# Strassen's identity in the second product of six feed-forward blocks, with the residual in DRAM meanwhile

## Chip, cores and metric

One core of a Trainium2 chip runs the whole kernel. The metric is the device time of one execution in microseconds (us), as the median of several runs. Engines: PE multiplies matrices (PEld loads its weights), DVE, ACT and POOL work elementwise, SP only issues DMAs.

## The reference

Two layers over a sequence of 1024 frames with 1024 channels, float32: layer 0 mixes with a convolution, layer 1 with retention, and each is followed by a feed-forward part. The change lies in the feed-forward part of layer 1:

```
h = modulate(rmsnorm(x, norm_mlp_g[i]), sh2, sc2)
x = x + g2[:, None, :] * (jnp.square(jax.nn.relu(h @ mlp_w1[i])) @ mlp_w2[i])
...
return rmsnorm(x, final_norm_g)
```

mlp_w1 is 1024 x 4096, mlp_w2 is 4096 x 1024, g2 is a gain for each channel.

## The kernel before

x lies in SBUF transposed: `self.x[n][t]` holds 128 channels (n = 0 to 7) by 512 frames (t = 0, 1, the halves of the sequence). To keep float32's precision every operand is split into a high part, rounded to fp32r, and a low part, the rest. `mm3` (L253) multiplies two such operands by three matmuls with 512 columns: high by high, high by low, low by high.

The hidden 4096 channels are worked in eight blocks `fb` of 512. `mlp` (L417) does for each block two products. The first: for each of four hidden tiles f, one weight block of 128x1024 (`block`, L235: a DMA of 512 KB to a raw tile on SP's queue, a cast to the high part on ACT, L245, and a subtraction for the low part on DVE, L246, both into whl tiles), then for each half 8 x 3 matmuls into one PSUM tile, Relu on ACT (L432), the square on DVE (L434), and the split into a packed hid tile (`split_pack`, L276: ACT L281, DVE L282). The second: for each pair np_ of output tiles one weight block, and for each of the two tiles and each half 4 x 3 matmuls into a PSUM tile, which DVE multiplies by g2 and adds to x in SBUF (L454).

`run` (L1160) calls `mlp` for layer 1 three times: block 0 for the first half of the frames, while the second half's retention ends (L1191); the norm of the second half (L1195) and blocks 1 to 7 for both halves (L1196); and block 0 for the second half, with the final norm of both halves and the stores of the output (L1207). Layer 0's feed-forward part uses the same weight layout through `layer_conv`, `mlp` and `mlp_split`.

A scheduler orders this part when the kernel is built: it lists the instructions of each engine by estimated durations and by the place in the program, so an engine may take a later instruction that is ready before an earlier one that is not; on the chip each engine runs its list in that order. A tile waits for a free buffer of its tag: raw 2, tmp 4, whl 8, hB 16, hid0 and hid1 5 each in this part, x0 and x1 8 each (x itself), PSUM 6 for products. A raw tile is free when the cast and the subtraction have read it.

Of the kernel before, what the change touches and what calls it, by code (L numbers as in the profile page):

```python
# [6 lines left out]
F32 = mybir.dt.float32  # L7
F32R = mybir.dt.float32r
BF16 = mybir.dt.bfloat16
AF = mybir.ActivationFunctionType  # L10
ALU = mybir.AluOpType
PSUM = bass.MemoryType.PSUM

P = 128
D = 1024
S = 1024
HALF = 512
KT = D // P
# [7 lines left out]
MID = HALF // 2  # L26

VEC = {}


def _vec_layout():
# [175 lines left out]
class Trunk:  # L207
# [209 lines left out]
    def mlp(self, layer, sched, h, g2, mid=None, split=None):  # L417
        nc, io = self.nc, self.io
        for fb, halves in sched:
            hid = {t: [] for t in halves}  # L420
            for f in range(4):
                w = self.block(io["w1"][layer, fb * 4 + f])
# [19 lines left out]
            for np_ in range(4):  # L442
                w = self.block(io["w2"][layer, fb, np_])
                if self.bg:
                    self.bg.pop(0)()
                for n2 in range(2):
                    n = np_ * 2 + n2
                    for t in halves:
                        ps = self.psum()
                        for kt in range(4):  # L450
                            o = kt * 256 + n2 * P
                            self.mm3(ps, w, o, hid[t][kt], kt == 0, kt == 3)
                        x = self.x[n][t]
                        nc.vector.scalar_tensor_tensor(x, ps, g2[:, n : n + 1], x, ALU.mult, ALU.add)  # L454

    def mlp_split(self, layer, fb, t, hid, g2, done):

        nc = self.nc
        ws = [self.block(self.io["w2"][layer, fb, np_]) for np_ in range(4)]
        for cs in (slice(0, MID), slice(MID, HALF)):  # L460
            for n in range(KT):
                ps = self.psum()[:, :MID]
                for kt in range(4):
                    o = kt * 256 + n % 2 * P
                    self.mm3(ps, ws[n // 2], o, [a[:, cs] for a in hid[kt]], kt == 0, kt == 3)
                x = self.x[n][t][:, cs]
                nc.vector.scalar_tensor_tensor(x, ps, g2[:, n : n + 1], x, ALU.mult, ALU.add)
            done(t, cs)


    def layer_conv(self):
# [324 lines left out]
        def mlp(fb, p):  # L796
# [15 lines left out]
            for np_ in range(4):  # L812
                name = ("w2", fb, np_)
                for n in (2 * np_, 2 * np_ + 1):
                    ps, x = ("psw", fb, n), ("y", n, 0)
                    for kt in range(4):
                        mm(ps, name, kt * 256 + n % 2 * P, hid[kt], kt == 0, kt == 3, p)
                    op("V", 0.663, p, lambda ps=ps, x=x, n=n: nc.vector.scalar_tensor_tensor(
                        E[x][:, :HALF], E[ps], c1(("modb", 5), n), E[x][:, :HALF], ALU.mult, ALU.add), r=[ps, ("modb", 5)], w=[x])

# [339 lines left out]
    def run(self):  # L1160
# [22 lines left out]
        with tc.tile_pool(name="ret", bufs=1, reuse_waits="tile") as rp, tc.tile_pool(name="dp", bufs=1, space=bass.MemoryType.DRAM) as dp:  # L1183
# [5 lines left out]
            hm = {0: h0}  # L1189
            self.hidtag = {0: ["q", "k"]}  # L1190
            self.mlp(1, [(0, [0])], hm, g2, mid=out)  # L1191
        with tc.tile_pool(name="g1", bufs=1, reuse_waits="tile") as gp:
            self.tags.update(whl=(gp, 8), hB=(gp, 16), hid0=(gp, 5), hid1=(gp, 5))
            self.hidtag = {0: ["hid0"], 1: ["hid1"]}
            hm[1] = self.norm(1, G2, sh2, "hB")  # L1195
            self.mlp(1, [(fb, [0, 1]) for fb in range(1, 8)], hm, g2)  # L1196

            def first():
                self.tagname = {"tmp": "hid0", "xg": "hA"}
# [38 lines left out]
def lay_out(i):  # L1238
# [11 lines left out]
    def kblocks(w):  # L1250

        k, nn = w.shape
        return w.reshape(k // 512, 4, P, 4, 256).transpose(0, 3, 2, 1, 4).reshape(k // 512, 4, P, 1024)

    vec = np.zeros((P, NVEC), np.float32)

    def put(name, a):
# [26 lines left out]
        "rgate": c(ktiles(win[:, 4096:], 0)),  # L1284
        "rout": c(kblocks(i["ret_w_out"][0])),
        "w1": c(np.stack([ktiles(w, 0) for w in i["mlp_w1"]])),
        "w2": c(np.stack([kblocks(w) for w in i["mlp_w2"]])),
    }
    d.update(constants_np())
    return d  # L1290
# [23 lines left out]
```

## Time and profile before

| | |
|---|---|
| median of 3 runs | 2702.75 us (2698.78 to 2705.78) |
| profiled execution | 2705.48 us |
| span of its trace | 2703.6 us |
| PE busy | 2613.8 us, 97% of the span, 11450 matmuls |
| DVE busy | 1635.2 us, 60% |
| ACT busy | 1068.3 us, 40% |
| POOL busy | 314.5 us, 12% |
| mean granted clock of PE | 0.985 of full speed |

Busy shares are means over the whole span. Matmuls are pipelined, so one matmul's own duration is longer than the distance to the next one. Blocks 1 to 7 of layer 1 fill the span from about 2026 to 2640 us. Durations of elementwise operations are in ns for one instruction; "idle before" is how long the engine had nothing to do ahead of these instructions, and behind the arrow stands what ended the wait.

### The profile page before, as it was taken

The numbers are of one execution on the slowest core, as the hardware profiler recorded it, in microseconds if no ns is written. First come the engines' busy times: TensorE is split into PE (matmuls) and PEld (weight loads), VectorE is DVE, ScalarE is ACT, GpSimd is POOL, SyncE is SP. The second block draws the span as 40 slices with busy tenths as digits, with TensorE's granted clock in tenths as the row PEclk, the third lists the DMA queues.
The fourth block names the chain that finished last, engine by engine and source line by source line (L and its number), as shares of the span: only waits on it lengthen the run. The fifth ranks groups of instructions, "written<-read, shape, count | busy, mean of one in ns | idle before, by whom it ended". The sixth has DMA issues, their size and how long they took to land.

```text
span 2703.6 us, 29259 instructions
## 1 busy us (share of the span) xinstructions
PE 2613.8 (97%) x11450; PEld 2119.2 (78%) x11450; DVE 1635.2 (60%) x2237; ACT 1068.3 (40%) x1582; POOL 314.5 (12%) x212
## 2 busy tenths in 40 slices
PE   2989999999999999999999999999999999999997
PEld 1756777888787888788888888888888888888886
DVE  7799999965577445645545655365565333333336
ACT  4656866463222323343433633433543211222124
POOL 3677439100000000000000000000000000000002
PEclk6999999999999999999999999999999999999999
DMA  7522322242376223322222232232222111111112
GB/s 253 203 71 86 109 93 87 93 128 98 119 233 217 96 94 96 115 86 94 71 94 94 71 103 85 71 101 86 78 70 71 48 54 47 47 47 47 48 54 86
DMA packets 77197, 259.66 MB, mean 96 GB/s; under 512 B 8577, under 2 KB 11009, under 8 KB 76930
## 3 DMA queue, kind: packets, MB, share of 16 engines
q1 hardware_dynamic: 74240, 252.98, 28.6%
q10 hardware_dynamic: 2818, 4.81, 0.5%
q8 instruction: 90, 1.47, 0.2%
q14 instruction: 49, 0.40, 0.0%
HBM read 251.46 MB, written 6.29 MB: 95 GB/s over the span
## 4 chain that ended last, share of the span: by engine, by line
PE 84%; DVE 7%; DMA 4%; ACT 2%; issue 2%; POOL 1%; DVEq 0%; ACTq 0%; SPq 0%; POOLq 0%
PE mm L260 25%; PE mm L259 25%; PE mm L258 25%; DMA araw<-ada 3%; PE mm L964 2%; PE mm L963 2%; PE mm L962 2%; DVE acc L733 1%; POOL cacc L741 1%; DVE whl L523 1%; DVE araw L319 1%; PE ax L606 1%; PE acc L721 1%; DVE araw L555 0%; DVE hid L555 0%
## 5 line engine op out<-in xcount | busy, mean ns | idle before, releaser
L245 ACT CAST whl<-raw 128x1024 fp32r<-128x1024 f32 x264 | 277.0, 1050 | 809.7 <-PE mm L259 472.3
L246 DVE TENSOR_TENSOR whl<-raw,whl 128x1024 fp32r<-128x1024 f32 x264 | 322.7, 1223 | 403.5 <-ACT whl L245 302.7
L258 PE MATMUL mm<-hA,whl 128*128 128x512 f32 x1200 | 483.2, 403 | 44.5 <-ACT whl L522 41.7
L260 PE MATMUL mm<-hA,whl 128*128 128x512 f32 x1200 | 475.5, 396 | 8.5 <-DVE whl L523 6.3
L259 PE MATMUL mm<-hA,whl 128*128 128x512 f32 x1200 | 476.1, 397 | 1.9 <-DVE hA L542 1.7
L258 PE MATMUL mm<-hid,whl 128*128 128x512 f32 (+1 forms) x1024 | 394.3, 386 | 4.6 <-ACT hid L281 3.0
L259 PE MATMUL mm<-hid,whl 128*128 128x512 f32 (+1 forms) x1024 | 392.8, 384 | 1.1 <-DVE hid L282 1.0
L260 PE MATMUL mm<-hid,whl 128*128 128x512 f32 (+1 forms) x1024 | 392.8, 384 | 0.0
L258 PEld LDWEIGHTS mm<-hA,whl 128*128 128x128 f32 x1200 | 227.7, 190 | 101.3 <-ACT whl L522 43.5
L258 PE MATMUL mm<-hB,whl 128*128 128x512 f32 x704 | 279.3, 397 | 0.0
L260 PEld LDWEIGHTS mm<-hA,whl 128*128 128x128 f32 x1200 | 227.5, 190 | 63.8 <-DVE whl L523 9.8
L259 PE MATMUL mm<-hB,whl 128*128 128x512 f32 x704 | 274.4, 390 | 0.0
L260 PE MATMUL mm<-hB,whl 128*128 128x512 f32 x704 | 274.2, 390 | 0.0
L259 PEld LDWEIGHTS mm<-hA,whl 128*128 128x128 f32 x1200 | 227.6, 190 | 58.7 <-issue 5.3
L454 DVE SCALAR_TENSOR_TENSOR x<-mm,modb,x 128x512 f32<-128x512 f32 x192 | 143.8, 749 | 211.6 <-PE mm L260 211.0
L741 POOL TENSOR_TENSOR cacc<-cacc,prod 128x512 f32<-128x512 f32 x166 | 253.4, 1529 | 112.9 <-ACT prod L738 57.9
L1143 POOL TENSOR_SCALAR hA<-x,vec 128x256 f32<-128x256 f32 (+1 forms) x12 | 7.5, 622 | 2164.3 <-DVE x L454 2143.8
L258 PEld LDWEIGHTS mm<-hid,whl 128*128 128x128 f32 x1024 | 192.9, 189 | 45.6 <-ACT hid L281 5.9
L259 PEld LDWEIGHTS mm<-hid,whl 128*128 128x128 f32 x1024 | 192.9, 188 | 41.3 <-DVE hid L282 2.9
L260 PEld LDWEIGHTS mm<-hid,whl 128*128 128x128 f32 x1024 | 193.1, 189 | 37.1
L733 DVE SCALAR_TENSOR_TENSOR acc<-x,vec,acc 128x512 f32<-128x512 f32 x239 | 166.8, 746 | 2.8 <-PE acc L721 1.9
L259 PEld LDWEIGHTS mm<-hB,whl 128*128 128x128 f32 x704 | 132.2, 188 | 31.3 <-issue 2.9
(233 smaller groups left out, 3776.3 us busy)
## 6 DMA issues: line engine op xcount, KB each, us to landing
raw<-w SPq DMA_DIRECT2D x192, 512.0 KB, 3.5
araw<-ada SPq DMA_DIRECT2D x80, 512.0 KB, 4.3
raw<-pw SPq DMA_DIRECT2D x38, 512.0 KB, 4.1
raw<-rqk SPq DMA_DIRECT2D x32, 512.0 KB, 3.5
raw<-rv SPq DMA_DIRECT2D x32, 512.0 KB, 3.5
raw<-rgate SPq DMA_DIRECT2D x32, 512.0 KB, 3.5
raw<-rout SPq DMA_DIRECT2D x32, 512.0 KB, 3.5
x<-x SPq DMA_DIRECT2D x32, 256.0 KB, 3.2
```

Source lines behind the costliest of these rows:

```text
L245: nc.scalar.copy(hi[i], raw[:, i * W : i * W + W])
L246: nc.vector.tensor_tensor(lo[i], raw[:, i * W : i * W + W], hi[i].bitcast(F32), ALU.subtract)
L258: nc.tensor.matmul(out, whi, rhi, start=start, stop=False)
L259: nc.tensor.matmul(out, whi, rlo, start=False, stop=False)
L260: self.last_mm = nc.tensor.matmul(out, wlo, rhi, start=False, stop=stop)
L319: i = nc.vector.scalar_tensor_tensor(raw, raw, 1.0, self.cond, ALU.mult, ALU.mult, accum_out=out)
L454: nc.vector.scalar_tensor_tensor(x, ps, g2[:, n : n + 1], x, ALU.mult, ALU.add)
L733: op("V", 0.68, p, lambda s=s, a=a: nc.vector.scalar_tensor_tensor(E[a], sl(s), wv(s), E[a], ALU.mult, ALU.add), r=[u], w=[a])
L741: op("G", 1.28, p, lambda pr=pr: nc.gpsimd.tensor_tensor(E[ca], E[ca], E[pr], ALU.add), r=[pr], w=[ca])
L962: nc.tensor.matmul(vps[jt], hh[0], wh, start=kt == 0, stop=False)
L963: nc.tensor.matmul(vps[jt], hh[0], wl, start=False, stop=False)
L964: nc.tensor.matmul(vps[jt], hh[1], wh, start=False, stop=kt == KT - 1)
```

## The change

For blocks 1 to 6 of layer 1 `mlp` is replaced by `mlp_seven`; block 7 and block 0 stay as they were.

- The second product of a pair of output tiles (n1, n2) is a product of 2 x 2 parts: the weights by output tile and by parity kj of the hidden tile, the hidden values by kj and by half of the frames. Strassen's identity in Winograd's form does it with seven products (`seven`) in place of eight. Each is summed over the two pairs p of hidden tiles, 2 x 3 matmuls into one PSUM tile.
- `pair_weights` makes the seven weight parts from one raw block: four sums and differences of 256 columns on DVE, and the high and low parts in four whl tiles (A11, A12, S1, S2 in one couple, S4, S3, A22 in the other). It replaces `block` there.
- In the first product both Relu (in place in PSUM) and Square are on ACT, the result going to an x0 tile. Of each p's four results (kj, t) it packs seven operands: B11, T1, B21, B22, T2, T3, T4, with four differences on DVE.
- The seven products are gathered with g2 into a tmp tile and three ev tiles: two activations on ACT and eight operations on DVE for each pair. The four sums are added to the residual by accumulating DMAs from POOL's queue into sixteen DRAM tiles xd of 256 KB.
- Ahead of block 1, x is stored to xd from SP's queue; after block 6 it is loaded again, the first half into x0 tiles, the second into halves of four hid0 tiles. In between, x1 tiles hold half of the second half's h.
- Buffers in this part: hB 8, hid0 14 (no hid1), q2 1, ev 6.
- w2's columns lie in another order in DRAM for both layers (`kpairs`, and `o2` in the readers); bytes and DMAs are the same.

```diff
+def o2(kt, n):
+    return (n % 2 * 4 + kt % 2 * 2 + kt // 2) * P
...
+    def pair_weights(self, ap):
+        nc = self.nc
+        tt = nc.vector.tensor_tensor
+        raw = self.t2("raw", cols=1024)
+        nc.sync.dma_start(raw, ap)
+        a11, a12, a21, a22 = (raw[:, i * 256 : i * 256 + 256] for i in range(4))
+        ph, pl, qh, ql = (self.t2("whl", dt=F32R, cols=1024) for _ in range(4))
+        q = self.t2("q2")
+        tt(q[:, 256:], a11, a21, ALU.subtract)
+        nc.scalar.copy(qh[:, 512:768], a22)
+        tt(ql[:, 512:768], a22, qh[:, 512:768].bitcast(F32), ALU.subtract)
+        tt(a21, a21, a22, ALU.add)
+        tt(a22, a21, a11, ALU.subtract)
+        tt(q[:, :256], a12, a22, ALU.subtract)
+        nc.scalar.copy(ph, raw)
+        tt(pl, raw, ph.bitcast(F32), ALU.subtract)
+        nc.scalar.copy(qh[:, :512], q)
+        tt(ql[:, :512], q, qh[:, :512].bitcast(F32), ALU.subtract)
+        p, q = (ph, pl), (qh, ql)
+        return dict(A11=(p, 0), A12=(p, 256), S1=(p, 512), S2=(p, 768), S4=(q, 0), S3=(q, 256), A22=(q, 512))
+
+    def seven(self, np_, w, hid, g2, xd):
+        nc = self.nc
+        n1, n2 = 2 * np_, 2 * np_ + 1
+        g = lambda n: g2[:, n : n + 1]
+        def prod(a, k):
+            ps = self.psum()
+            wt, o = w[a]
+            for p in range(2):
+                self.mm3(ps, wt, o + p * P, hid[p][k], p == 0, p == 1)
+            return ps
+        def plus(ps, n, e, new=False):
+            o = self.t2("ev") if new else e
+            nc.vector.scalar_tensor_tensor(o, ps, g(n), e, ALU.mult, ALU.add)
+            return o
+        def done(n, t, e):
+            nc.gpsimd.dma_start(xd[n][t], e, accum_op=ALU.add)
+        ps = prod("A11", "B11")
+        a, b = self.t2("tmp"), self.t2("ev")
+        nc.scalar.activation(a, ps, AF.Copy, scale=g(n1))
+        nc.scalar.activation(b, ps, AF.Copy, scale=g(n2))
+        done(n1, 0, plus(prod("A12", "B21"), n1, a, True))
+        ps = prod("S2", "T2")
+        plus(ps, n1, a)
+        plus(ps, n2, b)
+        m5 = prod("S1", "T1")
+        plus(m5, n1, a)
+        plus(prod("S4", "B22"), n1, a)
+        done(n1, 1, a)
+        plus(prod("S3", "T3"), n2, b)
+        done(n2, 1, plus(m5, n2, b, True))
+        plus(prod("A22", "T4"), n2, b)
+        done(n2, 0, b)
+
+    def mlp_seven(self, layer, fbs, h, g2, xd):
+        nc, io = self.nc, self.io
+        tt = nc.vector.tensor_tensor
+        for fb in fbs:
+            hid = []
+            for p in range(2):
+                f = {}
+                ops = {}
+                pack = lambda k, src: ops.update({k: self.split_pack(src, "hid0")})
+                for kj in range(2):
+                    w = self.block(io["w1"][layer, fb * 4 + 2 * p + kj])
+                    for t in range(2):
+                        ps = self.psum()
...
+                        nc.scalar.activation(ps, ps, AF.Relu)
+                        sq = f[kj, t] = self.t2("x0")
+                        nc.scalar.activation(sq, ps, AF.Square)
+                        if (kj, t) == (0, 0):
+                            pack("B11", sq)
+                        elif (kj, t) == (0, 1):
+                            tt(f[0, 0], sq, f[0, 0], ALU.subtract)
+                            pack("T1", f[0, 0])
+                        elif (kj, t) == (1, 0):
+                            pack("B21", sq)
+                        else:
+                            pack("B22", sq)
+                            tt(f[0, 0], sq, f[0, 0], ALU.subtract)
+                            pack("T2", f[0, 0])
+                            tt(f[0, 1], sq, f[0, 1], ALU.subtract)
+                            pack("T3", f[0, 1])
+                            tt(f[1, 0], f[1, 0], f[0, 0], ALU.subtract)
+                            pack("T4", f[1, 0])
+                hid.append(ops)
+            for np_ in range(4):
+                self.seven(np_, self.pair_weights(io["w2"][layer, fb, np_]), hid, g2, xd)
...
-            self.tags.update(whl=(gp, 8), hB=(gp, 16), hid0=(gp, 5), hid1=(gp, 5))
-            self.hidtag = {0: ["hid0"], 1: ["hid1"]}
-            hm[1] = self.norm(1, G2, sh2, "hB")
-            self.mlp(1, [(fb, [0, 1]) for fb in range(1, 8)], hm, g2)
+            self.tags.update(whl=(gp, 8), hB=(gp, 8), hid0=(gp, 14), q2=(gp, 1), ev=(gp, 6))
+            self.hidtag = {t: ["hid0"] for t in range(2)}
+            xd = [[xp.tile([P, HALF], F32, name=self.nm("xd"), tag=f"xd{n}_{t}") for t in range(2)] for n in range(KT)]
+            r = self.norm_rstd(1)
+            h = []
+            for kt in range(KT):
+                nc.sync.dma_start(xd[kt][1], self.x[kt][1])
+                h.append(self.norm_h(1, kt, r, G2[:, kt : kt + 1], sh2[:, kt : kt + 1], "hB" if kt < 4 else "x1"))
+            hm[1] = h
+            for kt in range(KT):
+                nc.sync.dma_start(xd[kt][0], self.x[kt][0])
+            self.mlp_seven(1, range(1, 7), hm, g2, xd)
+            xl = [self.t2("hid0", cols=2 * HALF) for _ in range(4)]
+            for kt in range(KT):
+                self.x[kt][0] = self.t2("x0")
+                nc.sync.dma_start(self.x[kt][0], xd[kt][0])
+            for kt in range(KT):
+                self.x[kt][1] = xl[kt // 2][:, kt % 2 * HALF : kt % 2 * HALF + HALF]
+                nc.sync.dma_start(self.x[kt][1], xd[kt][1])
+            self.mlp(1, [(7, [0, 1])], hm, g2)
```

## Rows read from the trace of the kernel before

**Rows 1.** The head of the page and its busy times: busy us, share of the span, number of instructions of each engine.

```profile
span 2703.6 us, 29259 instructions
PE 2613.8 (97%) x11450; PEld 2119.2 (78%) x11450; DVE 1635.2 (60%) x2237; ACT 1068.3 (40%) x1582; POOL 314.5 (12%) x212
```

**Rows 2.** The table of stretches for three successive blocks, each cut into its first and its second product: stretch and length, busy us (and instructions) of each engine, granted clock of PE, busy share of the DMA engines, GB/s.

```profile
core 0: us, PE busy (x) PEld busy (x) DVE busy (x) ACT busy (x) POOL busy (x), PEclk, DMA share, GB/s
2115.06:2159.24 44.18, 44.18 (x193) 36.04 (x192) 15.07 (x19) 12.45 (x19) 0.00 (x0) 1.00 0.15 48
2159.24:2202.77 43.53, 43.53 (x194) 36.04 (x193) 17.36 (x21) 5.29 (x6) 0.00 (x0) 1.00 0.15 49
2202.77:2246.95 44.18, 44.18 (x193) 36.04 (x192) 15.05 (x19) 12.45 (x19) 0.00 (x0) 1.00 0.15 48
2246.95:2290.48 43.53, 43.53 (x194) 36.05 (x193) 17.35 (x21) 5.29 (x6) 0.00 (x0) 1.00 0.15 49
```

**Rows 3.** The same table for the instructions on hid tiles alone, in one second product.

```profile
2159.24:2202.77 43.53, 43.52 (x192) 35.85 (x191) 0.68 (x1) 0.62 (x1) 0.00 (x0) 1.00 0.15 49
```

**Rows 4.** PE's waits from 2000 to 2540 us, the one row of that answer: who waited for whom, us in total, times, the longest.

```profile
PE mm L260 <- DVE whl L246: 0.7, 1, 0.7
```

**Rows 5.** Groups of instructions on DVE and ACT from 2100 to 2537 us, shapes apart: busy us and mean ns of one, then idle time before them.

```profile
L454 DVE SCALAR_TENSOR_TENSOR x<-mm,modb,x 128x512 f32<-128x512 f32 x79 | 59.3, 750 | 123.1 <-PE mm L260 122.8
L246 DVE TENSOR_TENSOR whl<-raw,whl 128x1024 fp32r<-128x1024 f32 x40 | 49.0, 1225 | 73.7 <-ACT whl L245 71.5
L245 ACT CAST whl<-raw 128x1024 fp32r<-128x1024 f32 x40 | 41.9, 1048 | 248.6 <-PE mm L259 248.6
L282 DVE TENSOR_TENSOR hid<-tmp,hid 128x512 fp32r<-128x512 f32 x40 | 27.6, 691 | 24.0 <-ACT hid L281 24.0
L281 ACT CAST hid<-tmp 128x512 fp32r<-128x512 f32 x40 | 24.8, 621 | 43.0 <-DVE tmp L434 43.0
L432 ACT ACTIVATE tmp<-mm 128x512 f32<-128x512 f32 x40 | 23.8, 596 | 58.2 <-PE mm L260 58.2
```

**Rows 6.** The same view from 2600 to 2704 us, the end of the run: operations with 256 columns, and two on 512 columns from SBUF.

```profile
L1132 DVE TENSOR_TENSOR hid<-hid,hid 128x256 f32<-128x256 f32 x12 | 5.2, 437 | 0.7 <-ACT hid L1125 0.2
L1125 ACT ACTIVATE hid<-x 128x256 f32<-128x256 f32 x16 | 6.4, 412 | 13.8 <-DVE x L467 12.9 <-DVE hid L1132 0.7
L1151 DVE TENSOR_TENSOR hA<-hA,rs 128x512 f32<-128x512 f32 x5 | 6.3, 1319 | 0.0
L1132 DVE TENSOR_TENSOR hid<-hid,hid 128x512 f32<-128x512 f32 x7 | 5.1, 733 | 1.6 <-PE mm L260 0.7 <-ACT hid L1125 0.6
```

**Rows 7.** DVE's instructions in order of time around the end of a first product (at 2159.24): start, us, instruction, and in brackets the idle time before it and who ended it.

```profile
2156.06 0.69 DVE L282 TENSOR_TENSOR hid<-tmp,hid 128x512 fp32r<-128x512 f32 x1 [0.69 <-ACT hid L281]
2160.30 1.23 DVE L246 TENSOR_TENSOR whl<-raw,whl 128x1024 fp32r<-128x1024 f32 x1 [3.55 <-ACT whl L245]
2161.44 0.68 DVE L434 SCALAR_TENSOR_TENSOR tmp<-mm,tmp 128x512 f32<-128x512 f32 x1
2162.17 0.75 DVE L454 SCALAR_TENSOR_TENSOR x<-mm,modb,x 128x512 f32<-128x512 f32 x1
2162.84 0.68 DVE L282 TENSOR_TENSOR hid<-tmp,hid 128x512 fp32r<-128x512 f32 x1
```

**Rows 8.** ACT's instructions in the same stretch.

```profile
2159.22 1.05 ACT L245 CAST whl<-raw 128x1024 fp32r<-128x1024 f32 x1 [3.19 <-PE mm L259]
2160.17 0.59 ACT L432 ACTIVATE tmp<-mm 128x512 f32<-128x512 f32 x1
2162.16 0.62 ACT L281 CAST hid<-tmp 128x512 fp32r<-128x512 f32 x1 [1.40 <-DVE tmp L434]
```

**Rows 9.** DMA issues of the whole run by line: tiles, issuing queue, count, KB each, median us from issue to landing.

```profile
raw<-w SPq DMA_DIRECT2D x192, 512.0 KB, 3.5
std<-tmp SPq DMA_DIRECT2D x8, 256.0 KB, 2.0
tmp<-std SPq DMA_DIRECT2D x8, 256.0 KB, 2.6
```

**Rows 10.** The table of stretches where the first half's block 0 ends (to 2026) and the norm of the second half is made.

```profile
2004.00:2026.00 22.00, 22.00 (x98) 18.02 (x96) 9.29 (x12) 4.61 (x5) 0.00 (x0) 1.00 0.15 48
2026.00:2050.00 24.00, 23.35 (x100) 18.24 (x99) 21.91 (x31) 14.79 (x22) 0.00 (x0) 1.00 0.32 100
```

**Rows 11.** The longest wait of SP's queue from 2000 us on: the next weight load waits until DVE has read the raw tile.

```profile
SPq L239 <- DVE whl L246: 632.6, 65, 15.7
```

**Rows 12.** POOL's groups over the whole run: operations on two SBUF tiles of 512 columns.

```profile
L741 POOL TENSOR_TENSOR cacc<-cacc,prod 128x512 f32<-128x512 f32 x166 | 253.4, 1529 | 112.9 <-ACT prod L738 57.9 <-ACT cacc L738 43.7
L1151 POOL TENSOR_TENSOR hA<-hA,rs 128x512 f32<-128x512 f32 x3 | 4.7, 1593 | 27.7 <-DVE rs L374 27.7
```

More of the change, by code (lines that the diff above doesn't have):

```diff
@@ L450, in mlp @@
                         for kt in range(4):
-                            o = kt * 256 + n2 * P
-                            self.mm3(ps, w, o, hid[t][kt], kt == 0, kt == 3)
+                            self.mm3(ps, w, o2(kt, n), hid[t][kt], kt == 0, kt == 3)
                         x = self.x[n][t]
                         nc.vector.scalar_tensor_tensor(x, ps, g2[:, n : n + 1], x, ALU.mult, ALU.add)
+    def pair_weights(self, ap):
[18 more added lines that the diff above has]
+        return dict(A11=(p, 0), A12=(p, 256), S1=(p, 512), S2=(p, 768), S4=(q, 0), S3=(q, 256), A22=(q, 512))
@@ new lines, in mlp_seven @@
+    def mlp_seven(self, layer, fbs, h, g2, xd):
[12 more added lines that the diff above has]
+                        for kt in range(KT):
+                            self.mm3(ps, w, kt * P, h[t][kt], kt == 0, kt == KT - 1)
+                        nc.scalar.activation(ps, ps, AF.Relu)
[19 more added lines that the diff above has]
+                self.seven(np_, self.pair_weights(io["w2"][layer, fb, np_]), hid, g2, xd)
@@ L463, in mlp_split @@
                 for kt in range(4):
-                    o = kt * 256 + n % 2 * P
-                    self.mm3(ps, ws[n // 2], o, [a[:, cs] for a in hid[kt]], kt == 0, kt == 3)
+                    self.mm3(ps, ws[n // 2], o2(kt, n), [a[:, cs] for a in hid[kt]], kt == 0, kt == 3)
                 x = self.x[n][t][:, cs]
@@ L816, in mlp @@
                     for kt in range(4):
-                        mm(ps, name, kt * 256 + n % 2 * P, hid[kt], kt == 0, kt == 3, p)
+                        mm(ps, name, o2(kt, n), hid[kt], kt == 0, kt == 3, p)
                     op("V", 0.663, p, lambda ps=ps, x=x, n=n: nc.vector.scalar_tensor_tensor(
@@ L1191, in run @@
             self.mlp(1, [(0, [0])], hm, g2, mid=out)
+        xp = ctx.enter_context(tc.tile_pool(name="xd", bufs=1, space=bass.MemoryType.DRAM))
         with tc.tile_pool(name="g1", bufs=1, reuse_waits="tile") as gp:
-            self.tags.update(whl=(gp, 8), hB=(gp, 16), hid0=(gp, 5), hid1=(gp, 5))
-            self.hidtag = {0: ["hid0"], 1: ["hid1"]}
-            hm[1] = self.norm(1, G2, sh2, "hB")
-            self.mlp(1, [(fb, [0, 1]) for fb in range(1, 8)], hm, g2)
+            self.tags.update(whl=(gp, 8), hB=(gp, 8), hid0=(gp, 14), q2=(gp, 1), ev=(gp, 6))
[14 more added lines that the diff above has]
+                nc.sync.dma_start(self.x[kt][0], xd[kt][0])
+            for kt in range(KT):
+                self.x[kt][1] = xl[kt // 2][:, kt % 2 * HALF : kt % 2 * HALF + HALF]
+                nc.sync.dma_start(self.x[kt][1], xd[kt][1])
+            self.mlp(1, [(7, [0, 1])], hm, g2)
             def first():
@@ L1253, in kblocks, with kpairs @@
         return w.reshape(k // 512, 4, P, 4, 256).transpose(0, 3, 2, 1, 4).reshape(k // 512, 4, P, 1024)
+    def kpairs(w):
+        k, nn = w.shape
+        return w.reshape(k // 512, 2, 2, P, 4, 2, P).transpose(0, 4, 3, 5, 2, 1, 6).reshape(k // 512, 4, P, 1024)
     vec = np.zeros((P, NVEC), np.float32)
@@ L1286, in lay_out @@
         "w1": c(np.stack([ktiles(w, 0) for w in i["mlp_w1"]])),
-        "w2": c(np.stack([kblocks(w) for w in i["mlp_w2"]])),
+        "w2": c(np.stack([kpairs(w) for w in i["mlp_w2"]])),
     }
```

## Prediction

> **What bounds the kernel now.** I read first the page's line of busy times: PE is busy 97% of the span, DVE 60%, ACT 40%, POOL 12% [rows 1]. An average over unlike stages prices nothing, so the next view is the table of stretches, cut where a block's first product ends and its second ends [rows 2]. Three successive blocks look alike: 44.18 us for the first product, 43.53 us for the second, PE busy for all of both at granted clock 1.00. DVE works 15.1 and 17.4 us in them, ACT 12.5 and 5.3 us, POOL nothing, and the DMA engines are 0.15 busy at 48 GB/s. The same table for the instructions on the hid tiles alone counts 192 matmuls in the second product [rows 3], so one matmul costs 43.53/192 = 226.7 ns there; the first product has as many, at 44.18/192 = 230.1 ns. Last, the waits: in the 540 us from 2000 on PE waited once, 0.7 us [rows 4], while DVE's additions to x wait for PE [rows 5]. In these blocks the time is the count of matmuls and nothing else; the question is whether the new side work stays under PE.
>
> **What is removed.** A pair of output tiles takes 2 x 2 x 4 x 3 = 48 matmuls now and 7 x 2 x 3 = 42 afterwards: seven products, each over the two halves of the hidden block, three matmuls each. Per block 168 for 192, over six blocks 144 fewer: 144 x 0.2267 = **-32.7 us**. The second product becomes 168 x 0.2267 = 38.1 us, the block 82.3 us for 87.7, one pair 9.52 us, one product 1.36 us. Bound on the rate: products of 6 matmuls instead of 12 could run at the first product's 230.1 ns, 168 x 3.4 ns x 6 = 3.4 us; at or below the old rate costs 0. I take the middle, **+1.7**.
>
> **DVE and ACT.** Durations by form are in [rows 5]; the 256-column ones come from the tail of the run [rows 6]. On DVE a block has, in the first product, 4 weight subtractions at 1.225, 14 low halves of packs at 0.691 and 8 differences (nearest row the same 0.691) = 20.1 us. A pair's weights need five 256-column operations at 0.43 (four differences or sums and one low half), one of 1.225 and one of 0.69 = 4.1 us. A pair's results need eight evacuations at 0.750 = 6.0 us. Together 20.1 + 4 x 10.1 = 60.5 us of 82.3, 73%. ACT: 4 x 1.05 + 16 x 0.6 + 14 x 0.621 + 4 x (0.41 + 1.05 + 0.62) + 8 x 0.6 = 35.6 us, 43%; Relu written back to PSUM is in no row, and I take L432's 0.596. So neither is the bound over a block. It is tight inside the second product: 4 x 6.0 + 3 x 4.1 + 2 x 1.225 = 38.7 us of DVE against 38.1 of PE, if no pair is prepared earlier than it must be. It can be: the eight whl tiles hold two pairs, the first pair fits into the first product, and A11, A12, S1 and S2 of a pair are let go after its fourth product, so a pair's weights are wanted some 13 us after they can begin. Moving one pair's 4.1 us gives 34.6. Cost 0; the cover is DVE's idle time in the first product, and if it were gone the 0.6 us per block would cost 3.6 us in all.
>
> **The handover from first to second product.** The part most likely to cost. Now the last hidden tile is ready 4.3 us after its last matmul: the first product ended at 2159.24, ACT took a weight cast first and began the Relu at 2160.17, DVE ended the last low half at 2163.52 [rows 7, 8]. The first 12-matmul group and three quarters of the second hid that. Afterwards the chain is Relu 0.6, Square 0.6, difference 0.69, copy 0.62, low half 0.69 = 3.2 us, up to 5.0 with the 0.93 us of the cast and B22's 0.69 ahead and some 0.2 of hand-overs, up to 6.8 if DVE's weight subtraction and one more low half come between. PE wants T2's second half after two products and three matmuls, 3.4 us, or 4.8 us if S1*T1, ready long before, is issued ahead of S2*T2. So 0 to 3.4 us per block. I take 0.7, near the low end because a product with ready operands exists and the order is laid out from estimated durations: **+4.2** in six blocks (bounds 0 and 20.4).
>
> **The residual in DRAM.** 16 accumulating DMAs of 256 KB per block, issued from POOL, which otherwise does nothing here. No row shows an accumulating DMA or any issued from POOL. 48 GB/s at share 0.15 [rows 2] is 320 GB/s at full share, so a plain 256 KB transfer occupies the engines 0.82 us: the lower bound. The upper one is a load and a store of the same size that follow one another to the landing, 2.6 + 2.0 = 4.6 us [rows 9]. I take a read and a write side by side, 1.6 us, nearer the low end because successive DMAs go to different tiles and nothing makes one wait for another. Neither end reaches the path. On average 16 x 4.6 = 73.6 us fit into 82.3. Inside the second product the six ev tiles come round after two pairs, and the latest, n2's sum, must land within 19.0 + 1.4 - 9.5 = 10.9 us. With 4.6 us one after another the fourth pair finds two tiles 4.4 and 3.6 us late; DVE stands there, with the later evacuations and weight work queued behind it, and PE goes on over the free ones of six PSUM tiles, some four products or 5.4 us. Cost 0. The Trainium skill, Collectives: The Full Stack, section The bandwidth ceiling, says that an add in the DMA path reads two sources and so runs at half a copy's rate; no row here shows it. By it a DMA would take some 1.6 us as an estimate, and the sum would stay as it is.
>
> **Entry and exit.** The norm of the second half is hidden today: in the 24 us from 2026 PE lost 0.65 us [rows 10] while DVE was busy 21.9. Sixteen stores of 256 KB join SP's queue among the weight loads, and half of h waits for x1 tiles to be stored. SP waits only for free raw tiles [rows 11], so it has room. Bounds 0 and two stores in a row, 4.0 us; I take **+1.0**, nearer 0 since x is final up to 20 us before h is made. At the exit SP holds sixteen loads behind the last accumulations; a weight block is wanted each 11 us with two raw tiles ahead, and x itself only at the second product, 44 us later. Bounds 0 and 4.6, taken **+1.0**.
>
> **Sum.** -32.7 + 1.7 + 4.2 + 1.0 + 1.0 = -24.8 us. The profiled execution took 2705.48 us (span 2703.6), 2.7 above the median of 2702.75. 2705.5 - 24.8 = 2680.7 for an execution like it, and **2678** for the median.
>
> **Rivals.** *Eaten up:* all bounds at their upper ends, handovers 20.4, rate 3.4, entry 4.0, exit 4.6, together 32.4: -0.3, about 2702. For it: the handover chain grows while its cover shrinks from 12-matmul groups to 6-matmul ones. Against it: the ready product S1*T1, and six PSUM tiles.
>
> *Slower, the accumulating queue:* each DMA goes alone, read then write, 4.6 us, with POOL's issuing in front, nearest row the shortest two-input POOL operation on 512 columns, 1.529 [rows 12]: 6.1 us. 16 x 6.1 = 97.6 us per block becomes the period, 9.9 above today's 87.7, six times = +59, 2762. From 16 x t = 82.3, t = 5.1 us, the queue sets the time; from 5.5 us the change loses. For it: no row shows such a DMA. Against it: 0.15 of the DMA engines in use, and different targets.
>
> *Slower, DVE against POOL:* beside POOL's multiplications a DVE operation on two SBUF tiles took 1.319 us where the same size took 0.733 [rows 6, 12]. If each of 16 issues per block caught one so, DVE gains 9.4 us per block; the second product holds 38.7 + 9.4 - 4.1 = 44.0 of DVE for 38.1 of PE, +35.4 in six blocks: -24.8 + 35.4, 2713. Against it: that row's operations may be slow by their own form, and an issue reads no tile. The Trainium skill, SBUF - State Buffer, section SBUF: two separate sides, speaks against this change here: GpSimd cannot write the descriptors of its DMAs while DVE holds the ports that they share. Its rule is for DVE operations in a two-port mode; whether these are, no row shows.
>
> *Not what it says:* matmuls in groups of 6 at 43.53/168 = 259 ns would give nothing, 2703. Against it, the 227 ns hold everywhere in the steady blocks.
>
> **How the numbers follow.** Chances: forecast 0.64, eaten up 0.19, queue 0.10, DVE against POOL 0.04, not what it says 0.03. 0.3% is 8.1 us, about what a measurement of this kernel tells from no change. Faster: 0.64 and 0.08 of the eaten-up cases that keep over 8 us = 0.72. Same: 0.11 + 0.03 = 0.14. Slower: 0.14. Low end: -32.7 with nothing on the path, and half the spread of the three runs, 3.5 us, is 2666. High end: the eaten-up case with part of that scatter, 2704.
>
> **What would show it.** 168 matmuls per second product in some 38.1 us at 227 ns; blocks of some 83 us; PE's waits at the handover under 1 us each, S1*T1 ahead of S2*T2 where T2 is late; DVE some 60 us per block; accumulations that land under 5 us. Wrong: PE waiting for evacuations in the second product, DVE waiting for ev tiles or POOL's queue, a handover above 2 us, a stall where x goes to DRAM or comes back.

## The result, and the profile after

| | before | after |
|---|---|---|
| median (lowest to highest), 5 runs each | 2702.75 us (2698.78 to 2705.78) | 2688.67 us (2684.62 to 2691.75) |
| ratio, 95% interval | | 0.9948 [0.9933, 0.9962] |
| profiled execution, span | 2705.48, 2703.6 us | 2684.62, 2682.8 us |

The change makes the kernel 14.1 us faster (10 to 18 by the interval). The forecast was 2678 in 2666 to 2704: sign and range hold, and the forecast is 10.7 us too low. The head of the page after, with the busy times, answers to [rows 1]:

```profile
span 2682.8 us, 29885 instructions
PE 2583.2 (96%) x11306; PEld 2089.1 (78%) x11306; DVE 1771.8 (66%) x2513; ACT 1167.7 (44%) x1762; POOL 398.0 (15%) x308
```

PE has exactly 144 matmuls fewer. Where the time went is read from stretches cut at the first matmul of a product. The same table as [rows 2], of after and with its columns, for one block's first product and its second:

```profile
2104.83:2149.16 44.33, 44.33 (x193) 36.07 (x192) 20.29 (x34) 18.20 (x31) 2.62 (x3) 1.00 0.26 60
2149.16:2187.54 38.38, 38.38 (x169) 31.46 (x168) 34.26 (x52) 16.37 (x25) 11.31 (x13) 1.00 0.78 150
```

Against [rows 2] the first product takes 0.15 us more, the second 5.15 less; PE stays busy at granted clock 1.00, although DVE is now busy 34.26 of 38.38 us (89%) and the DMA engines 0.78. So the steady blocks do what was forecast. The rest of the run doesn't. The same view cut from block 1 to the end, columns as above; the five stretches are the six changed blocks, block 7, the last block's first product, from the first matmul behind it (before, one of the norm's) to DVE's last group of multiplications, and the end. Before:

```profile
2025.79:2553.59 527.80, 527.15 (x2306) 432.43 (x2305) 209.86 (x262) 115.26 (x157) 0.00 (x0) 1.00 0.16 51
2553.59:2641.30 87.71, 87.71 (x386) 72.09 (x384) 34.80 (x44) 24.13 (x35) 3.07 (x4) 1.00 0.14 49
2641.30:2663.06 21.76, 21.76 (x97) 18.02 (x96) 11.86 (x15) 9.89 (x15) 0.00 (x0) 1.00 0.23 73
2663.06:2697.11 34.05, 26.81 (x203) 24.86 (x201) 27.09 (x48) 16.14 (x36) 12.08 (x13) 0.99 0.26 94
2697.11:2703.60 6.49, 0.00 (x0) 0.00 (x0) 2.96 (x3) 0.00 (x0) 1.67 (x1) 0.50 0.48 162
```

And after:

```profile
2020.98:2519.99 499.01, 497.19 (x2161) 405.01 (x2161) 342.54 (x533) 214.55 (x336) 81.02 (x93) 1.00 0.50 105
2519.99:2607.87 87.88, 87.88 (x386) 72.11 (x384) 36.30 (x46) 21.38 (x29) 5.38 (x7) 1.00 0.33 98
2607.87:2629.82 21.95, 21.95 (x98) 18.01 (x96) 9.54 (x11) 7.59 (x11) 0.00 (x0) 1.00 0.24 72
2629.82:2674.49 44.67, 28.40 (x203) 25.77 (x201) 31.73 (x54) 21.33 (x45) 13.67 (x13) 0.79 0.20 72
2674.49:2682.80 8.31, 0.00 (x0) 0.00 (x0) 2.96 (x3) 0.00 (x0) 1.70 (x1) 0.50 0.38 126
```

Row by row: -28.79, +0.17, +0.19, **+10.62**, +1.82, together -15.99 us. The six blocks gave 28.8 us, more than the 24.8 of the forecast's whole sum, and 12.4 were given back behind block 0's first product, in a part that the sum doesn't mention. (The two spans differ by 20.8; the other 4.8 arose before block 1. Its first matmul starts anywhere from 2016.9 to 2025.8 us over the profiled executions of all kernels here, so single executions are compared by stretches below, not by spans.)

What waits in the fourth stretch shows in PE's waits from 2630 us on in before, and from 2600 us on in after. Before:

```profile
PE ax L1135 <- DVE hid L1132: 2.9, 2, 1.6
```

After (L1237 and L1234 are the same lines of the code, moved down):

```profile
PE ax L1237 <- DVE hid L1234: 13.5, 2, 8.9
```

These are the final norm's sums of squares. ACT makes the squares; in order of time, its first one of the first half of the frames before (L1125), behind a pack:

```profile
2600.69 0.62 ACT L281 CAST hid<-tmp 128x512 fp32r<-128x512 f32 x1 [1.39 <-DVE tmp L434]
2601.48 0.64 ACT L1125 ACTIVATE hid<-x 128x512 f32<-128x512 f32 x1 [0.17 <-DVE x L454]
```

After (L286 is the pack's cast, L1227 the square):

```profile
2632.73 0.62 ACT L286 CAST hid<-tmp 128x512 fp32r<-128x512 f32 x1 [1.39 <-DVE tmp L439]
2633.26 2.19 ACT L1227 ACTIVATE hid<-x 128x512 f32<-128x512 f32 x4
```

Before, the first square starts 39.8 us ahead of the end of block 7 (2641.30), as soon as DVE has finished that tile of x. The second waits for PE until 2636.74, since block 7's matmuls still read the buffers of hid0; the last two end at 2643.4, 2.1 us behind block 7:

```profile
2642.23 1.14 ACT L1125 ACTIVATE hid<-x 128x512 f32<-128x512 f32 x2
```

After, none starts until 25.4 us behind the end of block 7 (2607.87), right behind the last pack of block 0, though x's first half is final at 2606.1. All eight then run within 6 us, the last one ends 31.2 us behind block 7, and the first half's norm falls into the second half's. The first half's squares have been in tag hid0 in both kernels; but the second half's packs of block 0 were in hid1, which the change removed.

### The profile page after: what moved, and what is told of

Its sections match the earlier page's. It is cut to its first block, busy times and chain, and to the rows that moved or that the text cites. A ratio compares the mean times of both kernels' runs of the same rounds, so it can differ in the third digit from the quotient of the medians.

```text
span 2682.8 us, 29885 instructions
## 1 busy us (share of the span) xinstructions
PE 2583.2 (96%) x11306; PEld 2089.1 (78%) x11306; DVE 1771.8 (66%) x2513; ACT 1167.7 (44%) x1762; POOL 398.0 (15%) x308
## 4 chain that ended last, share of the span: by engine, by line
PE 69%; issue 14%; DVE 7%; DMA 4%; POOL 3%; ACT 2%; DVEq 0%; ACTq 0%; POOLq 0%; SPq 0%
PE mm L264 20%; PE mm L263 20%; PE mm L265 20%; DMA araw<-ada 3%; POOL xd L501 3%; PE mm L1064 2%; PE mm L1066 2%; PE mm L1065 2%; DVE acc L835 1%; PE acc L823 1%; DVE araw L324 1%; DVE araw L657 1%; POOL cacc L843 1%; DVE whl L625 1%; PE ax L708 0%
## 5 line engine op out<-in xcount | busy, mean ns | idle before, releaser
L251 DVE TENSOR_TENSOR whl<-raw,whl 128x1024 fp32r<-128x1024 f32 x240 | 293.3, 1223 | 339.5 <-ACT whl L250 244.3
L250 ACT CAST whl<-raw 128x1024 fp32r<-128x1024 f32 x240 | 251.9, 1050 | 603.9 <-PE mm L264 206.7
L263 PE MATMUL mm<-hid,whl 128*128 128x512 f32 (+1 forms) x976 | 375.2, 385 | 4.3 <-ACT hid L286 3.0
L264 PE MATMUL mm<-hid,whl 128*128 128x512 f32 (+1 forms) x976 | 373.5, 384 | 1.2 <-DVE hid L287 1.2
L265 PE MATMUL mm<-hid,whl 128*128 128x512 f32 (+1 forms) x976 | 372.5, 383 | 0.0
L501 POOL DMA_DIRECT2D xd<-ev x72 | 64.2, 913 | 1879.5 <-DVE ev L497 1877.5
L263 PE MATMUL mm<-hB,whl 128*128 128x512 f32 x576 | 229.4, 398 | 0.0
L264 PE MATMUL mm<-hB,whl 128*128 128x512 f32 x576 | 225.0, 391 | 0.0
L265 PE MATMUL mm<-hB,whl 128*128 128x512 f32 x576 | 224.8, 390 | 0.0
L263 PEld LDWEIGHTS mm<-hid,whl 128*128 128x128 f32 x976 | 183.5, 188 | 46.0 <-ACT hid L286 8.6
L264 PEld LDWEIGHTS mm<-hid,whl 128*128 128x128 f32 x976 | 183.8, 188 | 39.4 <-DVE hid L287 3.1
L265 PEld LDWEIGHTS mm<-hid,whl 128*128 128x128 f32 x976 | 183.8, 188 | 35.6 <-issue 0.2
L625 DVE TENSOR_TENSOR whl<-raw,whl 128x1024 fp32r<-128x1024 f32 x92 | 122.7, 1340 | 36.1 <-PE mm L264 10.9
L624 ACT CAST whl<-raw 128x1024 fp32r<-128x1024 f32 x92 | 95.8, 1045 | 101.2 <-DMA raw<-w 42.9
```

The costliest lines, as they stand in the source:

```text
L250: nc.scalar.copy(hi[i], raw[:, i * W : i * W + W])
L251: nc.vector.tensor_tensor(lo[i], raw[:, i * W : i * W + W], hi[i].bitcast(F32), ALU.subtract)
L263: nc.tensor.matmul(out, whi, rhi, start=start, stop=False)
L264: nc.tensor.matmul(out, whi, rlo, start=False, stop=False)
L265: self.last_mm = nc.tensor.matmul(out, wlo, rhi, start=False, stop=stop)
L501: nc.gpsimd.dma_start(xd[n][t], e, accum_op=ALU.add)
```

## Experiments

The theory: with one hid tag the buffers go out in program order, so the squares, which come behind block 0's four packs in the program, get none before the last of them; that alone makes the 10.6 us. A mere lack of buffers is less likely: block 7's last matmul, the last reader of its eight hid tiles, ends at 2607.9, 25 us before the first square, and block 0 packs only four. No run changes the order alone. The rival: another part of the change (x's new tiles, transfers that run late) makes the last block slower, and another tag would not help. The later runs test the terms of the prediction. The ratios are against runs of before on the same chip.

**The final norm's temporaries in another tag.** Base: the changed kernel.

```diff
-                self.tagname = {"tmp": "hid0", "xg": "hA"}
+                self.tagname = {"tmp": "ev", "xg": "hA"}
```

(in `first` and in `rest`, where the same line stands)

> The changed kernel with one word changed: the temporary tiles of the final norm are taken from tag ev (six tiles, free by then) in place of hid0. The tail is the time from the first matmul of the last block (block 0, second half) to the end of the span: 62.3 us before the change, 74.9 after it. Theory, shared tag: after the change the final norm's temporaries stand in one tag with the last block's four packed hidden tiles, get their buffers behind them, and the first half's final norm starts some 30 us later than before. Then the tail falls back to 62 to 63 us and the median to about 2676 (12.4 below the changed kernel). Rival, place of the residual: the tail is longer because the second half of x lies in halves of hid0 tiles and comes from DRAM; then the tail stays at 75 us and the time at 2688.

Measured: 2674.63 us (2671.37 to 2677.93, 4 runs) against 2701.45, ratio 0.9901 [0.9888, 0.9915]. The table of its last three stretches:

```profile
2611.70:2633.66 21.96, 21.96 (x98) 18.01 (x97) 9.53 (x11) 7.86 (x12) 0.00 (x0) 1.00 0.24 73
2633.66:2667.71 34.05, 26.80 (x203) 24.85 (x201) 27.04 (x47) 15.85 (x36) 12.10 (x13) 1.00 0.26 94
2667.71:2676.10 8.39, 0.00 (x0) 0.00 (x0) 2.96 (x3) 0.00 (x0) 1.67 (x1) 0.51 0.37 125
```

Its first square, in ACT's order of time, is 39.8 us ahead of the end of block 7 again:

```profile
2571.89 0.63 ACT L1227 ACTIVATE ev<-x 128x512 f32<-128x512 f32 x1 [0.20 <-DVE x L458]
```

The fourth stretch is back at 34.05 us, the same as before to the hundredth, and PE's waits for the norm are 2.9 us again. The 10.6 us are the tag's. The longer end stays (8.39 us for 6.49).

**The other way round: the kernel before with one hid tag.** Ten buffers as before, nothing else changed.

```diff
-            self.tags.update(whl=(gp, 8), hB=(gp, 16), hid0=(gp, 5), hid1=(gp, 5))
-            self.hidtag = {0: ["hid0"], 1: ["hid1"]}
+            self.tags.update(whl=(gp, 8), hB=(gp, 16), hid0=(gp, 10))
+            self.hidtag = {0: ["hid0"], 1: ["hid0"]}
```

> The kernel before, with nothing of Strassen and no residual in DRAM, but with both halves' packed hidden tiles in one tag hid0 of ten tiles in place of hid0 and hid1 of five each. Theory, shared tag: the tail grows from 62.3 to 74 or 75 us and the time from 2703 to about 2715. Rival, place of the residual: x lies where it lay, so the tail stays 62.3 and the time 2703.

Measured: 2711.21 us (2710.16 to 2714.5, 5 runs), ratio 1.0036 [1.0023, 1.0049], +9.8. Its last three stretches:

```profile
2639.85:2661.61 21.76, 21.76 (x97) 18.02 (x96) 9.53 (x11) 7.57 (x11) 0.00 (x0) 1.00 0.23 73
2661.61:2706.22 44.61, 28.41 (x203) 25.76 (x201) 31.71 (x54) 21.34 (x45) 13.70 (x13) 0.80 0.20 72
2706.22:2712.70 6.48, 0.00 (x0) 0.00 (x0) 2.96 (x3) 0.00 (x0) 1.70 (x1) 0.50 0.48 162
```

The fourth stretch grows by 10.56 us, without Strassen's identity and without a residual in DRAM. The end stays at 6.48: the 1.8 us have another cause, and the expectation for the three stretches together (74 to 75, measured 72.85), which counted them in, was about that much too high.

**PE held in program order at the handover.** Base: the changed kernel. Each product's first matmul is held behind the previous product's last in PE's list, so S1*T1 can't go ahead of S2*T2's second half. One run.

```diff
-        nc.tensor.matmul(out, whi, rhi, start=start, stop=False)
+        self.first_mm = nc.tensor.matmul(out, whi, rhi, start=start, stop=False)
...
+            last = self.last_mm
             for p in range(2):
                 self.mm3(ps, wt, o + p * P, hid[p][k], p == 0, p == 1)
+                if p == 0 and a != "A11":
+                    self.after(last, self.first_mm)
```

> The changed kernel, with the matmuls of each product of a pair held behind those of the product before, so that S1*T1 cannot be taken while S2*T2 waits for its second operand. Theory, the handover costs nothing because S1*T1 fills it: in the changed kernel T2's low half is ready about 4.7 us after the last matmul of the first product, and in program order it is wanted after 2.7 + 0.7 + 0.2 = 3.6 us, so PE then stands 1.0 us per block, the second product takes 39.4 us for 38.38, and the time rises by 6 us to about 2695. Rival: the operand is ready in time and the order does not matter; then 38.4 and 2688.

Measured: 2687.98 us; the second product takes 39.32 to 39.33 us in all six blocks, 0.94 more than in blocks 1 to 5 of the changed kernel. PE in order of time, at the place where a first product has ended 4 us before:

```profile
2153.15 0.49 PE L263 MATMUL mm<-hid,whl 128*128 128x512 f32 x1 [0.21 <-ACT hid L286]
2154.09 0.50 PE L264 MATMUL mm<-hid,whl 128*128 128x512 f32 x1 [0.45 <-DVE hid L287]
```

PE waits twice for T2's second half, for the high part from ACT and for the low part from DVE. So the scheduler's mixed order (in the changed kernel's list three matmuls of S2*T2, then S1*T1's among the rest) is worth 0.94 us per block. The expected 2695 did not show in the single time of the whole run; from block 1's first matmul to the end 666.0 us pass instead of 661.9: five blocks lose 0.94 each, and block 6, with 39.97 in the changed kernel, gains 0.6.

**Half the ev tiles.** Base: the changed kernel. One run.

```diff
-            ... hid0=(gp, 14), q2=(gp, 1), ev=(gp, 6))
+            ... hid0=(gp, 14), q2=(gp, 1), ev=(gp, 3))
```

> The changed kernel with three ev tiles in place of six. Theory, six ev tiles are what hides the accumulating DMAs: they land 5.9 us (median) after the issue, and with three tiles each pair waits for the landing of the pair before; some 5 us late per pair, of which the six PSUM tiles hide the first, so the second product takes 48 to 53 us and the time is 2750 to 2780. Rival: landings are short enough against a pair's 9.5 us; then 38.4 us and 2688.

Measured: 2724.68 us. Second products take 41.8 to 45.6 us, first ones up to 46.97, a block about 88.7 us instead of 82.72: +36 us over the six, which is more than the whole gain. Waits from 2020 to 2560 us:

```profile
DVE ev L497 <- DMA xd<-ev: 57.7, 17, 6.0
PE mm L263 <- DVE ev L497: 17.7, 8, 3.9
```

The chain is the one of the prediction: DVE stands for an ev tile until its accumulating DMA has landed, and PE for DVE's evacuation. The direction was right, the expected size (2750 to 2780) too large; why the second products lost only 3 to 7 us no run shows. With six ev tiles no engine waits for a free one.

**Plain stores in place of the additions.** Base: the changed kernel. One run.

```diff
-            nc.gpsimd.dma_start(xd[n][t], e, accum_op=ALU.add)
+            nc.gpsimd.dma_start(xd[n][t], e)
```

> The changed kernel with plain stores in place of accumulating DMAs, from the same queue; the adding to the residual is left out, so the sums of earlier blocks are overwritten. Theory, the accumulation is off PE's path: first and second products stay 44.3 and 38.4 us and the time 2688 within 4 us, while the DMA engines' share in the second product falls from 0.78 to about 0.5 and the landing from 5.9 to about 3 us. Rival: the accumulations fill the DMA engines and so delay weights; then the products get shorter, by up to the 0.3 us per second product that is left over the count of matmuls.

Measured: 2683.83 us, just outside the expected 2688 within 4; from block 1's first matmul to the end 662.3 us, beside 661.9 with the additions. Steady blocks take 44.33 and 38.38 us, as with them. A second product in the table of stretches, beside the one of after above:

```profile
2147.72:2186.10 38.38, 38.38 (x170) 31.46 (x168) 36.03 (x54) 16.46 (x25) 7.55 (x14) 1.00 0.48 163
```

The DMA share falls from 0.78 to 0.48 and PE's time doesn't change. The DMA view from 2060 to 2520 us (queue: packets, MB, share of 16 engines; issues: count, KB each, median us to landing), after:

```profile
q0 software_dynamic: 13104, 23.86, 34.4%
raw<-w SPq DMA_DIRECT2D x44, 512.0 KB, 5.2
xd<-ev POOLq DMA_DIRECT2D x70, 256.0 KB, 6.1
xd<-tmp POOLq DMA_DIRECT2D x23, 256.0 KB, 5.3
```

And with plain stores:

```profile
q0 software_dynamic: 7515, 24.64, 13.8%
raw<-w SPq DMA_DIRECT2D x45, 512.0 KB, 3.6
xd<-ev POOLq DMA_DIRECT2D x72, 256.0 KB, 2.6
xd<-tmp POOLq DMA_DIRECT2D x24, 256.0 KB, 3.1
```

23.86 MB are 91 DMAs of 262144 bytes: 0.344 x 460 / 91 = 1.74 us of all 16 DMA engines for each addition; 0.138 x 460 / 94 = 0.675 us for a plain store. The weight loads beside the additions land in 5.2 us for 3.6.

**The exit: the loads of x from POOL's queue.** Base: the first experiment's kernel (temporaries in ev). In the changed kernel block 6's second product takes 39.97 us, 1.59 more than the others (in the base 39.62, 1.24 more). The lines are the changed kernel's. SP's queue there, in order of time, issues the loads of x's second half over 8.4 us, with the next weight load behind them:

```profile
2510.48 8.41 SPq L1314 DMA_DIRECT2D hid<-xd  x6
2518.99 0.38 SPq L244 DMA_DIRECT2D raw<-w  x1
```

And ACT's cast waits for a weight block, with an evacuation (L506) behind it for which PE waits:

```profile
2514.87 1.05 ACT L250 CAST whl<-raw 128x1024 fp32r<-128x1024 f32 x1 [5.90 <-DMA raw<-w]
2516.40 0.68 ACT L506 ACTIVATE ev<-mm,modb 128x512 f32<-128x512 f32 x1
```

```diff
-                nc.sync.dma_start(self.x[kt][0], xd[kt][0])
+                nc.gpsimd.dma_start(self.x[kt][0], xd[kt][0])
...
-                nc.sync.dma_start(self.x[kt][1], xd[kt][1])
+                nc.gpsimd.dma_start(self.x[kt][1], xd[kt][1])
```

> The first of these kernels (final norm's temporaries in ev), with the sixteen loads of x after block 6 issued from POOL's queue in place of SP's. Theory: the 1.6 us that the second product of block 6 is longer than those of blocks 1 to 5 (39.97 for 38.38) is SP's queue, in which weight loads stand behind loads of x that wait for the last accumulations; then it becomes 38.4 and the time falls by 1.6 us, to about 2674. Rival: the weight loads are late because the DMA engines are full in that stretch; then it stays near 40.0.

Measured: 2676.54 us (2673.91 to 2678.5, 4 runs), ratio 0.9908 [0.9894, 0.9921]. Block 6's second product takes 38.37 us: the stall is gone, with the same loads in another queue, so it wasn't that the DMA engines were full. The whole can't be told from the first experiment's 2674.63: from block 1's first matmul to the end both take 651.0 us, as this profile's end takes 9.65 us and that one's 8.39. With plain stores the stall is gone as well (38.38), though the loads of x stand on SP's queue and wait for the stores there. SP's waits in the changed kernel, from 2490 to 2560 us, and with plain stores, from 2480 to 2560 us:

```profile
SPq L1311 <- DMA xd<-ev: 33.7, 8, 8.3
SPq L1311 <- DMA xd<-ev: 24.6, 8, 7.1
```

So the loads of x wait for additions that land late, longer than for stores, and the weight loads stand behind them.

**Seven blocks instead of six.** Base: the first experiment's kernel.

```diff
-            self.mlp_seven(1, range(1, 7), hm, g2, xd)
+            self.mlp_seven(1, range(1, 8), hm, g2, xd)
...
-            self.mlp(1, [(7, [0, 1])], hm, g2)
```

> The first of these kernels (final norm's temporaries in ev), and block 7 by the seven products too, so that x is loaded again during block 0's second half. If a block is worth its 4.98 us wherever it stands, the time falls another 5 us, to about 2671, with a tail of 62 to 64 us. Rival: the reload has only the 22 us of the last first product as its cover, the first half's final norm starts later, and the tail takes back up to 5 us: 2676.

Measured: 2681.5 us (2678.74 to 2683.28, 5 runs), ratio 0.9925 [0.9912, 0.9937], slower than six blocks by some 7 us; theory (2671) and rival (2676) were both too low. The second product of block 7 takes 40.39 us in place of 43.55, but from block 0's first matmul on 72.59 us pass instead of 64.40. Waits from 2600 to 2640 us:

```profile
ACT whl L250 <- DMA raw<-w: 16.5, 3, 10.7
ACT ev L1227 <- DMA xd<-ev: 4.1, 1, 4.1
```

Block 7 is the cover of the loads of x. Without it SP's queue holds block 0's weights behind them, and the first half's norm comes late: POOL's part of it (L1245) waits 18.7 us for x in the same stretch. The second line is no wait for x: that square writes an ev tile, and starts as the addition from such a tile lands, at 2625.2. With seven blocks ev isn't free by then, so this run changes two things at once. The end, 9.66 us, takes 1.3 of the loss.

**Seven blocks, with the loads of x on POOL's queue.** Both edits above together.

> Seven blocks by the seven products, the final norm's temporaries in ev, and the loads of x from POOL's queue. With seven blocks and SP's queue the time was 2681.5: the last first product took 22.7 us and PE stood another 5 us behind weights and hidden tiles of the last block. Theory, SP's queue: weight loads no longer stand behind loads of x, the waits for weights go, and the block's 4.98 us come out: about 2671, 3 to 5 below the kernel with six blocks (2674.6). Rival: x itself comes too late for the first half's final norm, whoever issues its loads, and ACT and DVE hold the last block's hidden tiles behind it; then 2677 to 2682.

Measured: 2679.25 us (2674.23 to 2684.07, 4 runs), ratio 0.9922 [0.9904, 0.9939]; not to be told from the run before, and not better than six blocks, as the rival had it (2677 to 2682). Block 0's first product is back at 21.98 us, so the weights are no longer late; but block 7's second product takes 45.67, 7.3 more than the others. Two matmuls lie 4.86 us apart in one place, and the twelve behind them follow at 0.43 us in place of 0.23, at granted clock 0.52 (2599.04 to 2604.14). ACT's waits from 2580 to 2640 us:

```profile
ACT hA L1247 <- DMA x<-xd: 24.1, 3, 9.1
```

The final norm's work on ACT waits for x, in ACT's order ahead of an evacuation that PE needs (L506, at 2598.31 behind a wait of 9.06 for x). The reload moved its stall from one queue to another.

**One transfer from POOL's queue, in the kernel before.** For the end of the run, which is 1.8 us longer after the change: the load of a constant at the start goes through POOL's queue. One run.

```diff
-        nc.sync.dma_start(self.ident, io["ident"])
+        nc.gpsimd.dma_start(self.ident, io["ident"])
```

> The kernel before with one 64 KB constant loaded from POOL's queue in place of SP's, so that the program has one DMA from POOL and nothing else of the change. The time from the start of the last group of multiplications on DVE to the end of the span was 6.49 and 6.48 us in the two kernels without DMAs from POOL, and 6.8 to 10.6 in seven with them. If the mere use of POOL's DMA queue makes the program's end longer: 8 us or more. If it depends on what those DMAs did: 6.5 us. All else as in the kernel before, 2703 within 5 us.

Measured: 2702.33 us, with an end of 6.91 us. The two kernels with no DMA on POOL's queue end in 6.49 and 6.48 us, those with the residual in DRAM in 8.31 to 10.56, except the run with seven blocks and the loads on POOL's queue, with 6.79. Expected were 8 us or more, or 6.5; the one transfer gave 0.4 of the 1.8. Where the time is shows in the closing instructions of the program (L1299 before, L1423 after), which hold a DRAIN on POOL (count; shortest, median and longest ns; first and last start):

```profile
L1299 POOLq DRAIN  x3: 39/78/1767, 2697.2 to 2703.3; - x3
L1423 POOLq DRAIN  x3: 40/102/7493, 2674.6 to 2682.6; - x3
```

The longest starts beside POOL's last multiplication. Before, it is over at 2699.0, while SP still waits for the last stores, until 2702.9. After, it ends at 2682.1, 1.5 us behind SP's last wait, and the program's last instructions come behind it. It lasts 9.7 us with plain stores, 8.8 in the two kernels with 112 DMAs on POOL's queue, and 3.5 in the one with 128, whose end is 6.79. So 1.5 of the 1.8 us are this DRAIN's; what sets its length stays open.

## Why the prediction was right, and where it was not

**Matmuls and rate: right.** 168 x 0.2267 = 38.1 us was forecast, 38.38 measured. The terms for the rate (+1.7) and the handover (+4.2) were 5.9 us together and measured 0.30 us in each of six blocks, 1.8. The handover went as described. In DVE's order of time after, the first product having ended at 2149.16, three low halves of the block's last operands end by 2154.45, 5.3 us later, and T2's, the second of them in the program, some 4.7 us later; both lie inside the 3.2 to 6.8 of the forecast:

```profile
2151.36 0.68 DVE L549 TENSOR_TENSOR x<-x,x 128x512 f32<-128x512 f32 x1
2152.56 1.89 DVE L287 TENSOR_TENSOR hid<-x,hid 128x512 fp32r<-128x512 f32 x3
```

S1*T1 covers it, and the steady first products grew by 0.15 us each. The only wait of PE's two queues in this second product (2149.16 to 2187.54):

```profile
PEld mm L263 <- ACT hid L286: 0.4, 1, 0.4
```

Without that cover the run with PE in program order lost 0.94 us more per block: of 0 to 3.4 the forecast's 0.7 was too high for the order that the scheduler found, and about right for the other.

**DVE and ACT: right.** 60.5 us of DVE per block were forecast and 20.29 + 34.26 = 54.6 measured; ACT 35.6 and 34.6. Neither limits PE, though DVE is busy 89% of the second product.

**The residual in DRAM: cost 0 right, the landing outside its bounds.** One addition costs the engines 1.74 us (1.6 was taken), but it lands in a median of 5.9 us (below), and the upper bound was 4.6. The *accumulating queue* put its loss at 16 x t with t from 5.5 us on, and such a t was there; yet nothing was lost, because additions overlap: 13 issues in 38.38 us, at 5.9 each, are 77 us of landing. In time of the engines 16 additions take 16 x 1.74 = 28 of a block's 82.7 us; no run drove them to that limit. The Trainium skill, Collectives: The Full Stack, section The bandwidth ceiling, lets an add in the DMA path run at half a copy's rate, for the ring of a collective. The runs show 1.74 against 0.675 us for SBUF to DRAM on one core, a factor of 2.6.

**DVE against POOL: refuted.** Additions to ev tiles on DVE took 745 ns beside the issues and 750 before [rows 5], packs 688 against 691. POOL's issues from 2100 to 2192 us, most of them inside second products:

```profile
L501 POOL DMA_DIRECT2D xd<-ev x16: 862/865/1098, 2100.5 to 2190.8; - x16
DMA to landing us min/median/max: 3.8/5.9/8.6
```

An issue takes 862 ns at least, 865 in the median and 1098 at most, with DVE busy 89% of the second product. The blocking that the Trainium skill describes (SBUF — State Buffer, section SBUF: two separate sides) doesn't show with these operations.

**Entry and exit.** At the entry block 1's first product got 0.28 us shorter (45.75 to 45.47) and the two matmuls of the second half's norm ahead of it 0.61 longer (1.07 for 0.46): +0.3 for a forecast of 1.0. The exit cost 1.59 for 1.0, at the place named, SP's queue.

**The step that failed is the sum itself.** It ran over six blocks, their entry and their exit, and priced block 7, block 0 and the final norm at nothing without a reason; their code stays as it was. Their buffers didn't: the list of the change has "hid0 14 (no hid1)", and the norm's temporaries lie in hid0. The missing term is +10.6 us for the one tag (shown from both sides, 10.62 given back in the changed kernel and 10.56 caused in the one before; that it acts through the order in which the buffers go out is read from the trace), and +1.8 at the end (POOL's DRAIN for the most part, its length open). The forecast's -24.8, with -28.79 in the six blocks (the shorter first product and the exit are in it), +0.6 ahead of block 1, +0.4 in block 7 and block 0's first product and +12.4 behind it, becomes -15.4, beside -14.1 between the medians. "Eaten up", at 2702, had the right sort of outcome in the wrong place: 12.4 of 28.8 us went, hardly any of it at the handovers. That the time fell inside the range is in part luck: rate and handover, 4.1 us too dear, covered a third of the missing 12.4.

The better version is the first experiment's: the change with the norm's temporaries in ev, 2674.63 us, 0.9901 of before.

## What to carry to other kernels

When a change merges or resizes buffer tags, list everything that takes buffers of that tag, also in stages whose code is untouched, and ask in which program order they go out: with this scheduler a tile that is ready early waits behind all that stand ahead of it in the program. Before a work-saving step is spread to the last block of a stage, ask what that block hides (here the reload of x and half of the final norm). Keep a DMA's time to landing and its time of the engines apart: here they were 5.9 and 1.74 us, the first set how many buffers were needed (three ev tiles in place of six cost 36 us), and it was no limit on the rate.

## What the hardware showed that was not expected

- An accumulating DMA of 256 KB from SBUF to DRAM took 1.74 us of the 16 engines and landed in 5.9 us, a plain store of the same tiles 0.675 and 2.6 to 3.1 us. It also needs more packets, 13104 for 91 DMAs against 7515 for 94.
- PE's rate didn't suffer from it: 38.38 us per second product at a DMA share of 0.78 and of 0.48.
- In the fourth stretch PE's granted clock fell to 0.50, its level of 1.2 GHz, after PE had begun to wait for the sums of squares from DVE, which is busy for all of 2650 to 2655. The table of stretches there, after:

```profile
2650.00:2655.00 5.00, 4.07 (x34) 3.87 (x33) 5.00 (x7) 0.82 (x2) 2.68 (x2) 1.00 0.80 293
2655.00:2660.00 5.00, 1.22 (x2) 0.50 (x2) 3.48 (x9) 2.42 (x8) 1.54 (x3) 0.60 0.21 79
2660.00:2665.00 5.00, 0.00 (x0) 0.00 (x0) 3.57 (x6) 2.12 (x6) 2.27 (x2) 0.50 0.00 1
```

  For the same 203 matmuls PE is busy 28.40 us in place of 26.81: of the 10.6 us of the stretch 1.6 are these, and 9.0 are idle time of PE (44.67 - 28.40 against 34.05 - 26.81).
- The last stretch, from DVE's last group to the end, is 0.3 to 4.1 us longer in the kernels with the residual in DRAM. POOL's closing DRAIN lasts 3.5 to 9.7 us in them, for 1.8 before; no run settles what sets it.
